# Starting the state space tables' small operations 20 steps earlier, in the first half of the values' product

## The chip, the cores and the metric

One Trainium2 chip, one of its cores. The metric is the device time of one execution in microseconds (us). Before the change it is 940.51 us, the median of 3 runs from 940.02 to 942.69. Engine names in the rows: PE is TensorE (PEld its weight loads), DVE is VectorE, ACT is ScalarE, POOL is GpSimd, SPq is SyncE's DMA queue.

## What is computed

One layer of an encoder on 512 tokens of 1024 channels. The parts that matter here:

```python
xn = rmsnorm(h, norm_mix)
proj = xn @ w_in                       # channels for S5, pooling, q, k, v, gates
u_s5, u_pool, qkv, gate_logits = split(proj)

dt = exp(log_dt)[:, None]              # S5: 64 rows (2 directions x 32 groups) of 64 states
a_bar = exp(lam * dt)                  # complex
b_bar = ((a_bar - 1.0) / lam)[:, :, None] * b
# a scan over time with a_bar, then a product with c

scores = einsum('bdiqhe,bdikhe->bdihqk', q, k) - slopes * dist
p = exp(scores - max(scores))          # dilated attention, 16 heads
```

Behind them follow the merge of the three branches by their gates, an output projection and a two-layer network.

## The kernel before

**Products in three matmuls.** Every float32 operand of a large product is split into a high part (a rounded copy) and a low part (the difference), and `mm3` (lines 121 to 123) adds high x high, high x low and low x high. ScalarE makes the high half of a weight piece (`wh`, line 96), VectorE the low half (`wl`, line 103). Weight pieces are loaded by SyncE into three raw buffers (line 181). The load into a buffer is issued right behind the low split that empties it, in program order, so SyncE waits there for that split. Each of `wh` and `wl` has two buffers.

**Steps.** The order of all work is the order in which the program issues it, engine by engine. A clock counts steps: `tick()` (line 136) is called after each `mm3` group and issues what is due: first the calls put off with `later(n, f)`, then one portion of each generator in `background`. `use(i)` (line 235), called as a product reaches weight piece `i`, puts off the split of piece `i + 1`: its high half by two steps, its low half by three. `finish()` (line 154) ticks until no generator is left, without any matmul in between.

**The stretch of the change.**
- Steps 1 to 32: first half of the values' product (`tokmajor(P_v[0], ...)`, line 695). Its left operand is x scaled by the norm's gains, not yet by the rows' factors; `v_ahead` (line 441) splits x for a later channel block, and at `k == 1` (step 4) starts the generator `norm1`. Here `k` counts channel blocks of four steps, so `k == 3` is called with the clock at 12.
- `norm1` (line 383): loads x by rows (until step 11), squares them on ScalarE (steps 19 to 26), makes the rows' factors `rows_rs` on GpSimd (step 27), broadcasts them on VectorE (30) and transposes the broadcast on TensorE (step 32, line 409). From step 34 to 58 it does, for each of eight channel blocks in three steps each, a product on VectorE (`nx`: line 106), a copy on ScalarE (`xh`) and a difference on VectorE (`xl`).
- Steps 33 to 64: second half of the values' product (line 699). Low splits of weight pieces are issued in steps 35, 43, 51 and 59; the one of step 51 is first used in step 57, the one of step 59 by the first S5 unit.
- Steps 65 to 88: three units of the S5 input projection (line 719), eight steps each, with low splits in steps 67, 75 and 83. Steps 89 to 104: the units for k and q of the first two heads, whose results VectorE and ScalarE evict (`k_done`, `q_done`). Steps 105 to 108: half of the fourth S5 unit. Then `finish()` (line 956), the loads of the first two score bias tables T (`load_T`, line 751) and of the S5 tables; then the attention loop.

**The list of the change.** `s5_prep()` (line 450) makes the S5 tables: about 110 operations, nearly all on VectorE and on 64 partitions. It does not issue them as it runs; it records them with an estimated cost and then plays the list back, a portion per step:

```python
for cost, f in ops:
    if cost is None:
        spent = 0.0
        yield f
        continue
    f()
    spent += cost
    if spent > PACE:
        spent = 0.0
        yield
```

`PACE` is 0.35, so two small operations (0.2 or 0.22) go out per step, or one wide one. The order in the list: three loads and a pause of 8 steps; an exponential on 64 x 1 (15 operations); the products with dt and the two reduced angles; an exponential on 64 x 64 (15); two sines on ScalarE and a pause of 3; powers of a_bar by complex products of growing width (64 x 64 to 64 x 512); the factor (a_bar - 1) / lam; two products and two sums on 64 x 1024 or half of it; four stores to DRAM; eight loads; a pause of 16 (`PREP_WAIT`); 19 transposes on TensorE; their evictions; and six operations on 128 x 512 (`Bb`). Each score tile adds the bias table T on VectorE (line 770), and the softmax rows are normalised by GpSimd (line 109) before TensorE transposes them (line 797).

Of the kernel before, what the change touches and what calls it, by code (L numbers as in the profile page):

```python
# [55 lines left out]
def trunk(ctx: ExitStack, tc: tile.TileContext, a: dict, out):  # L56
# [7 lines left out]
    def fr(t):  # L64
        return t.bitcast(F32)
# [10 lines left out]
    def z(dt=F32, n=512):  # L76
        t = z_p.tile([128, 512], dt, tag="z", name="z")
        return t if n == 512 else t[:, 0:n]
# [4 lines left out]
    def ps():  # L83
        return ps_p.tile([128, 512], F32, tag="ps", name="ps")

    def sm(n=1):
        t = small.tile([128, 4], F32, tag="sm", name="sm")
        return t[:, 0:n]
# [5 lines left out]
    def copy(eng, o, i, scale=1.0):  # L94
        if eng is SE:
            SE.activation(out=o, in_=i, func=AF.Copy, scale=scale)  # L96
        elif scale != 1.0:
            eng.tensor_scalar(out=o, in0=i, scalar1=scale, scalar2=1.0, op0=MUL, op1=MUL)
        else:
            eng.tensor_copy(out=o, in_=i)  # L100

    def tt(o, i, j, op, eng=None):
        (eng or VE).tensor_tensor(out=o, in0=i, in1=j, op=op)  # L103

    def stt(o, i, s, j, op0, op1):
        VE.scalar_tensor_tensor(out=o, in0=i, scalar=s, in1=j, op0=op0, op1=op1)  # L106

    def ts(o, i, s1, s2, op0, op1, eng=None):
        (eng or VE).tensor_scalar(out=o, in0=i, scalar1=s1, scalar2=s2, op0=op0, op1=op1)  # L109
# [22 lines left out]
    def later(n, f):  # L132
        clock[1] += 1
        put_off.append((clock[0] + n, clock[1], f))
# [16 lines left out]
    def start(gen):  # L151
        background.append([clock[0] + 1, gen])
# [194 lines left out]
    def split_xT(k):  # L347
        h, l = xg_h[k], xg_l[k] = zr(), zr()
        g = gT[:, k:k + 1]
        SE.activation(out=h, in_=xT[k], func=AF.Copy, scale=g)  # L350
        stt(l, xT[k], g, fr(h), MUL, SUB)
# [31 lines left out]
    def norm1():  # L383

        xs = []
        for t in range(4):
            for hf in range(2):
                x = z()
                SP.dma_start(out=x, in_=a["x"][t * 128:t * 128 + 128, 512 * hf:512 * hf + 512])
                xs.append(x)  # L390
            yield 2
        yield 6
        for i, x in enumerate(xs):
            SE.activation(out=x, in_=x, func=AF.Square, accum_out=rows_ss[:, i % 2, i // 2:i // 2 + 1])
            yield 1
        s2 = sm(4)
        tt(s2, rows_ss[:, 0], rows_ss[:, 1], ADD, GE)
        ts(s2, s2, 1.0 / D, EPS, MUL, ADD, GE)
        mh4 = mhalf.to_broadcast([128, 4])
        tt(rows_rs, s2, mh4, ALU.pow, GE)  # L400
        yield 3
        rb = z()
        for t in range(4):
            ts(rb[:, t * 128:t * 128 + 128], ones, rows_rs[:, t:t + 1], 1.0, MUL, MUL)
        yield 2
        p = ps()
        for t in range(4):
            o = slice(t * 128, t * 128 + 128)
            TE.transpose(p[:, o], rb[:, o], ident)
        yield 1  # L410
        copy(SE, R, p)
        yield 1
        for k in range(8):
            stt(xT[k], xT[k], gT[:, k:k + 1], R, MUL, MUL)
            yield 1
            copy(SE, xT_h[k], xT[k])
            yield 2
            tt(xT_l[k], xT[k], fr(xT_h[k]), SUB)
# [3 lines left out]
    def v_evac(t, hf, p):  # L422
        vt[t][hf] = z()
        SE.activation(out=vt[t][hf], in_=p, func=AF.Copy, scale=rows_rs[:, t:t + 1])

    def tokmajor(P, lhs_h, lhs_l, ahead=None):

        acc = [ps() for _ in range(4)]
        ks = [(pi, i) for pi in P for i in range(pieces[pi][0].shape[1])]
        for k, (pi, i) in enumerate(ks):  # L430
            if i == 0:
                hs, ls = use(pi)
            if ahead:
                ahead(k)
            for t in range(4):
                o = slice(t * 128, t * 128 + 128)
                mm3(acc[t], lhs_h[k][:, o], lhs_l[k][:, o], hs[i], ls[i], k == 0, k == len(ks) - 1)
                tick()
        return acc

    def v_ahead(k):
        if k < 6:
            later(1, lambda: split_xT(k + 2))
        if k == 1:
            start(norm1())


    s5c = []
# [226 lines left out]
    def unit_quanta(pi, hT, lT, done, ks=range(8), sub=None):  # L675
# [17 lines left out]
        return [lambda i=i: quantum(i) for i in range(n)]  # L693

    acc0 = tokmajor(P_v[0], xg_h, xg_l, v_ahead)
    for t in range(4):
        later(1 + t, lambda t=t: v_evac(t, 0, acc0[t]))
    start(s5_prep())
    acc = tokmajor(P_v[1], xg_h, xg_l)
    for t in range(4):  # L700
        later(1 + t, lambda t=t: v_evac(t, 1, acc[t]))
# [933 lines left out]
```

## Time and profile before

| | us |
|---|---|
| median of 3 runs | 940.51 (940.02 to 942.69) |
| the profiled execution | 939.83 |
| its span, first to last instruction | 938.0 |
| TensorE busy | 918.2 (98%) |
| VectorE busy | 586.3 (63%) |
| ScalarE busy | 444.7 (47%) |
| GpSimd busy | 308.0 (33%) |

All rows come from the profiled execution, which was 0.68 us below the median; the span leaves out the 1.8 us around its first and last instruction. Busy shares are means over stages with different limits. A row of a timeline has the start, the length, the engine, the line of the kernel, the operation, the tiles written and read, a count and, in brackets, the idle time of the engine before it with what ended it. The length of a short row overlaps the next one: what an operation costs its engine is the distance from start to start. TensorE's granted clock stands as a fraction of 2.4 GHz; it is 1.00 in every row that is shown here.

### The profile page before, as it was taken

Reading aid. Unit: us, or ns where it says so; the run is one execution under the profiler, and the core shown is the slowest. Engines: PE = TensorE matmul, PEld = TensorE weight load, DVE = VectorE, ACT = ScalarE, POOL = GpSimd, SP = SyncE. Lnnn points to the kernel's source line nnn. Section 1 sums busy time; section 2 is a strip of 40 time slices with the busy share of each in tenths; the row PEclk is TensorE's granted clock in tenths of the full one; section 3 lists DMA queues with packets and bytes.
Section 4 is the critical chain, followed back from the end, with each engine's and each line's share of the span. In section 5 each row is a group of like instructions: output and inputs, shape, how many; then the busy total and the mean of one; then the engine's idle time right before and its main releaser. Section 6 shows DMA issues by size and latency. Waiting matters only on the chain.

```text
span 938.0 us, 12750 instructions
## 1 busy us (share of the span) xinstructions
PE 918.2 (98%) x4683; PEld 736.6 (79%) x4683; DVE 586.3 (63%) x921; ACT 444.7 (47%) x711; POOL 308.0 (33%) x416
## 2 busy tenths in 40 slices
PE   9999999999999999999999999999999999999997
PEld 6878776777777888878888878888888888888876
DVE  4698788887544765567754564436665857675443
ACT  5544765667654334444444332345444444444522
POOL 0000465557788883022100000056034314501302
PEclk9999999999999999999999999999999999999999
DMA  9237766642313334454352254281333134221222
GB/s 323 85 116 204 200 180 168 161 120 87 103 48 100 94 101 124 107 127 115 108 152 63 73 179 135 68 268 47 107 116 115 53 96 154 82 66 45 67 90 90
DMA packets 140462, 111.05 MB, mean 118 GB/s; under 512 B 16368, under 2 KB 117104, under 8 KB 140400
## 3 DMA queue, kind: packets, MB, share of 16 engines
q1 hardware_dynamic: 140400, 110.24, 39.6%
q8 instruction: 37, 0.61, 0.3%
q14 instruction: 25, 0.20, 0.1%
HBM read 106.32 MB, written 3.90 MB: 117 GB/s over the span
## 4 chain that ended last, share of the span: by engine, by line
PE 80%; DVE 11%; ACT 4%; issue 2%; DMA 1%; SPq 0%; POOLq 0%; DVEq 0%; POOL 0%; ACTq 0%
PE ps L121 20%; PE ps L122 20%; PE ps L123 20%; PE ps L1461 4%; PE ps L1462 4%; PE ps L1460 4%; DVE z L103 3%; PE ps L813 2%; DVE wl L103 2%; ACT z L96 2%; DVE z L106 2%; PE ps L797 2%; DVE S L770 1%; ACT wh L96 1%; PE ps L1131 1%
## 5 line engine op out<-in xcount | busy, mean ns | idle before, releaser
L103 DVE TENSOR_TENSOR wl<-raw,wh 128x1024 fp32r<-128x1024 f32 (+1 forms) x113 | 152.8, 1354 | 171.8 <-ACT wh L96 171.0
L121 PE MATMUL ps<-xh,wh 128*128 128x512 f32 x384 | 156.5, 407 | 0.2 <-ACT wh L96 0.2
L123 PE MATMUL ps<-xh,wl 128*128 128x512 f32 x384 | 150.3, 391 | 0.9 <-DVE wl L103 0.9
L122 PE MATMUL ps<-xl,wh 128*128 128x512 f32 x384 | 149.7, 390 | 0.0
L96 ACT ACTIVATE wh<-raw 128x1024 fp32r<-128x1024 f32 (+1 forms) x112 | 117.5, 1049 | 34.4 <-issue 9.3
L96 ACT ACTIVATE z<-ps 128x512 f32<-128x512 f32 (+4 forms) x128 | 72.8, 579 | 67.9 <-PE ps L123 25.2
L122 PE MATMUL ps<-hl,wh 128*128 128x512 f32 (+1 forms) x272 | 102.5, 377 | 0.3 <-DVE hl L103 0.3
L121 PE MATMUL ps<-hh,wh 128*128 128x512 f32 (+1 forms) x272 | 102.5, 377 | 0.3 <-ACT hh L96 0.3
L123 PE MATMUL ps<-hh,wl 128*128 128x512 f32 (+1 forms) x272 | 102.4, 376 | 0.0
L109 POOL TENSOR_SCALAR S<-S,sm 128x512 f32<-128x512 f32 x64 | 61.2, 974 | 97.6 <-ACT wh L96 78.4
L123 PEld LDWEIGHTS ps<-xh,wl 128*128 128x128 f32 x384 | 72.1, 188 | 17.0 <-DVE wl L103 1.3
L121 PEld LDWEIGHTS ps<-xh,wh 128*128 128x128 f32 x384 | 72.4, 189 | 14.9 <-issue 0.9
L122 PEld LDWEIGHTS ps<-xl,wh 128*128 128x128 f32 x384 | 72.4, 189 | 12.7
L1361 ACT ACTIVATE R<-ps 128x512 f32<-128x512 f32 x32 | 19.2, 598 | 128.0 <-PE ps L123 128.0
L103 POOL TENSOR_TENSOR z<-z 128x512 f32<-128x512 f32 x24 | 38.0, 1599 | 122.0 <-DVE z L106 75.8
L777 ACT ACTIVATE S<-S,sm 128x512 f32<-128x512 f32 x64 | 46.2, 722 | 53.9 <-DVE sm L109 52.2
L1460 PE MATMUL ps<-wh,ah 128*128 128x512 f32 x168 | 65.4, 389 | 0.0
L1461 PE MATMUL ps<-wh,al 128*128 128x512 f32 x168 | 65.4, 389 | 0.0
L1462 PE MATMUL ps<-wl,ah 128*128 128x512 f32 x168 | 65.4, 389 | 0.0
L109 POOL TENSOR_SCALAR sm<-sm 128x1 f32<-128x1 f32 (+1 forms) x16 | 3.6, 225 | 175.9 <-ACT hn L1331 148.1
L103 POOL TENSOR_TENSOR B<-B,B 128x1024 f32<-128x1024 f32 x18 | 50.4, 2820 | 27.9 <-DVE wl L103 16.1
L122 PEld LDWEIGHTS ps<-hl,wh 128*128 128x128 f32 x272 | 51.2, 188 | 10.0 <-DVE hl L103 0.5
(208 smaller groups left out, 1900.4 us busy)
## 6 DMA issues: line engine op xcount, KB each, us to landing
raw<-in_w_in_dram SPq DMA_DIRECT2D x55, 512.0 KB
raw<-in_w_up_dram SPq DMA_DIRECT2D x32, 512.0 KB
B<-in_w_down_dram SPq DMA_DIRECT2D x24, 512.0 KB
T<-in_ttab_dram SPq DMA_DIRECT2D x16, 448.0 KB
z<-Fd SPq DMA_DIRECT2D x16, 256.0 KB
raw<-in_w_branch_attn_dram SPq DMA_DIRECT2D x8, 512.0 KB
raw<-in_w_out_dram SPq DMA_DIRECT2D x8, 512.0 KB
raw<-in_w_down_dram SPq DMA_DIRECT2D x8, 512.0 KB
```

Of the source, the lines that this page charges most:

```text
L96: SE.activation(out=o, in_=i, func=AF.Copy, scale=scale)
L103: (eng or VE).tensor_tensor(out=o, in0=i, in1=j, op=op)
L106: VE.scalar_tensor_tensor(out=o, in0=i, scalar=s, in1=j, op0=op0, op1=op1)
L109: (eng or VE).tensor_scalar(out=o, in0=i, scalar1=s1, scalar2=s2, op0=op0, op1=op1)
L121: TE.matmul(o, wh, xh, start=first, stop=False)
L122: TE.matmul(o, wh, xl, start=False, stop=False)
L123: TE.matmul(o, wl, xh, start=False, stop=last)
L777: SE.activation(out=s, in_=s, func=AF.Exp, bias=nm, accum_out=den[h][:, t:t + 1])
L1361: SE.activation(out=r, in_=p, func=AF.Relu)
L1460: TE.matmul(acc[t], ah[:, k, o], hs[i], start=st, stop=False, **kw)
L1461: TE.matmul(acc[t], al[:, k, o], hs[i], start=False, stop=False, **kw)
L1462: TE.matmul(acc[t], ah[:, k, o], ls[i], start=False, stop=sp, **kw)
```

## The change

The generator `s5_prep` is started by `v_ahead` at channel block 3 of the first half of the values' product, with the clock at 12, and no longer between the two halves, with the clock at 32. Nothing else differs; the list, its pauses and its pace are the same.

```diff
@@ -443,6 +443,8 @@
             later(1, lambda: split_xT(k + 2))
         if k == 1:
             start(norm1())
+        if k == 3:
+            start(s5_prep())
 
 
     s5c = []
@@ -695,7 +697,6 @@
     acc0 = tokmajor(P_v[0], xg_h, xg_l, v_ahead)
     for t in range(4):
         later(1 + t, lambda t=t: v_evac(t, 0, acc0[t]))
-    start(s5_prep())
     acc = tokmajor(P_v[1], xg_h, xg_l)
     for t in range(4):
         later(1 + t, lambda t=t: v_evac(t, 1, acc[t]))
```

## Rows read from the trace of the kernel before

**Rows 1.** Busy time by 10 us: engines, granted clock, DMA share, GB/s.

```profile
20.00:30.00 10.00, 10.00 (x48) 8.31 (x47) 3.96 (x7) 7.00 (x19) 1.78 (x3) 1.00 0.62 212
...
40.00:50.00 10.00, 9.17 (x41) 7.27 (x40) 9.45 (x32) 3.48 (x5) 0.00 (x0) 1.00 0.31 91
```

**Rows 2.** TensorE's timeline, 40 to 62 us: start, length, instruction, [idle before, its releaser].

```profile
47.47 0.50 PE L122 MATMUL ps<-wl,z 128*128 128x512 f32 x1 [0.83 <-DVE wl L103]
...
54.78 0.51 PE L123 MATMUL ps<-xh,wl 128*128 128x512 f32 x1 [0.87 <-DVE wl L103]
...
60.37 0.39 PE L123 MATMUL ps<-xh,wl 128*128 128x512 f32 x1
```

**Rows 3.** Who waited for whom, TensorE, 0 to 200 us: total, times, longest.

```profile
PE ps L797 <- POOL S L109: 2.5, 7, 0.7
```

**Rows 4.** VectorE's timeline, 20 to 40 us.

```profile
25.73 1.23 DVE L103 TENSOR_TENSOR wl<-raw,wh 128x1024 fp32r<-128x1024 f32 x1 [3.26 <-ACT wh L96]
28.44 0.88 DVE L109 TENSOR_SCALAR z<-ones,rows_rs 128x128 f32<-128x128 f32 x4 [1.49 <-POOL rows_rs L103]
30.73 0.75 DVE L106 SCALAR_TENSOR_TENSOR z<-z,gT,R 128x512 f32<-128x512 f32 x1 [1.41 <-ACT R L96]
32.26 1.23 DVE L103 TENSOR_TENSOR wl<-raw,wh 128x1024 fp32r<-128x1024 f32 x1 [0.78 <-ACT wh L96]
...
35.45 0.69 DVE L103 TENSOR_TENSOR xl<-z,xh 128x512 fp32r<-128x512 f32 x1 [0.70 <-ACT xh L96]
...
38.45 1.23 DVE L103 TENSOR_TENSOR wl<-raw,wh 128x1024 fp32r<-128x1024 f32 x1 [1.04 <-ACT wh L96]
```

**Rows 5.** VectorE's timeline, 40 to 75 us.

```profile
46.21 1.21 DVE L103 TENSOR_TENSOR wl<-raw,wh 128x1024 fp32r<-128x1024 f32 x1
...
53.52 1.21 DVE L103 TENSOR_TENSOR wl<-raw,wh 128x1024 fp32r<-128x1024 f32 x1
...
56.66 0.19 DVE L476 MEMSET P<- 64x64 f32 x2
...
56.95 1.21 DVE L103 TENSOR_TENSOR wl<-raw,wh 128x1024 fp32r<-128x1024 f32 x1
...
59.81 0.42 DVE L103 TENSOR_TENSOR m<-P,sg 64x256 f32<-64x256 f32 x1
...
65.56 0.22 DVE L103 TENSOR_TENSOR sp<-sp,sp 64x64 f32<-64x64 f32 x1
...
72.13 2.44 DVE L103 TENSOR_TENSOR Fw<-m,m 32x1024 f32<-32x1024 f32 x2
```

**Rows 6.** SyncE's queue, 0 to 112 us.

```profile
17.30 0.94 SPq L389 DMA_DIRECT2D z<-in_x_dram  x2
...
86.63 1.06 SPq L753 DMA_DIRECT2D T<-in_ttab_dram  x2
```

**Rows 7.** Timeline of all engines, 26 to 31 us.

```profile
27.39 1.02 POOL L103 TENSOR_TENSOR rows_rs<-sm,mhalf 128x4 f32<-128x4 f32 x1
...
29.46 0.60 PE L409 MATMUL ps<-ident,z 128*128 128x128 f32 x4
```

**Rows 8.** Table operations on small tiles (sp) alone, 45 to 56.7 us.

```profile
45.00:56.70 11.70, 5.64 (x29) 0.39 (x2) 1.00 0.21 60
```

**Rows 9.** TensorE's timeline, 84 to 91 us.

```profile
84.75 1.16 PE L607 MATMUL ps<-ident,m 64*128 64x64 f32 x16
...
90.30 0.40 PE L767 MATMUL ps<-kz,z 128*128 128x512 f32 x1
```

**Rows 10.** VectorE's timeline, 92 to 125 us.

```profile
92.85 0.68 DVE L770 CUSTOM_DVE_ANT_0 S<-ps,T 128x512 f32<-128x512 f32 x1
...
120.92 1.66 DVE L103 TENSOR_TENSOR wl<-raw,wh 128x1024 fp32r<-128x1024 f32 x1
```

**Rows 11.** Busy time, GB/s last, as the tables for the first scores load.

```profile
87.00:90.00 3.00, 3.00 (x15) 2.47 (x14) 2.94 (x12) 1.08 (x2) 0.00 (x0) 1.00 0.82 260
90.00:91.00 1.00, 1.00 (x6) 0.79 (x5) 0.96 (x3) 0.98 (x3) 0.00 (x0) 1.00 0.99 373
```

## The prediction

> **What bounds the kernel now.** I first read the busy time in stretches of 10 us [rows 1]. TensorE is full from 20 to 30 us and loses 0.83 us from 40 to 50; VectorE goes the other way, 3.96 us busy in the first stretch and 9.45 in the second. So VectorE sets the pace in the second, and has room in the first. TensorE's own timeline shows what the loss is [rows 2]: it waits for the low half of a weight piece (a `wl` that VectorE makes), 0.83 us before 47.47 and 0.87 us before 54.78. The split after those two is early: its first use is at 60.37. Up to 200 us the list of waits names one other large item, transposes that wait for softmax rows normalised on GpSimd, 2.5 us in seven waits [rows 3]. Then VectorE's timeline: before 40 us its gaps, with the engine that ended each [rows 4], and the saturated stretch behind [rows 5]. An engine works in the order of issue, so what follows is a running account of one queue.
>
> **What is removed and added: nothing.** The same instructions are issued; the list of table operations starts 20 steps earlier (after step 12, not 32; a step is three matmuls, 0.68 us). Its three loads go out in step 13, its VectorE work starts in step 21 (before: 41) and it ends in step 102 (before: 122). The last 14 of the old steps held no matmul: `finish()` ran them after step 108.
>
> **Steps 21 to 30: hidden.** Eighteen small operations fall here, about 3.1 us, twelve before the `wl` at 25.73 and six after it. The gaps there are 3.26 and 1.49 us [rows 4]. They fit, if the loads have landed. On SyncE's queue these stand after the last x loads, issued from 17.30 to 18.24 [rows 6], so they are out by 20. The transfers ahead of them keep the DMA engines busy for about half of the stretch from 20 to 30 (share 0.62 [rows 1]); if all move in order of issue, the loads land near 23.3 us, and I take 0. If they land last, at 24.5, the eighteen end about 0.6 us late, and TensorE waits that long for the broadcast it transposes at 29.46 [rows 7].
>
> **Steps 30 to 64: the main term.** I go from one `wl` to the next and ask how late it is against before.
> - To the `wl` of step 43 (38.45). Steps 30 to 42 now carry 26 small operations instead of 4. Twenty-nine of them took 5.64 us busy, 0.194 each [rows 8], and with the gap to the next, some 0.02, one costs 0.215: 5.6 us in place of 0.7. The gaps they meet are 1.41, 0.78, 0.70 and 1.04, 3.9 us [rows 4]. Some 0.5 us of these stay idle, because the ScalarE copies that end them are bound to TensorE or to VectorE's own output. Late: 5.6 - 0.7 - 3.9 + 0.5 = 1.5 us; I take 1.4, as some operations overlap a neighbour.
> - To the `wl` of step 51 (46.21). Twelve operations: those that ran from 56.66 to 59.81 before [rows 5], less one `wl` of 1.14 from start to start, 2.0 us, and one more of 0.2; the list's pause for the sine leaves 0.5 idle. Before there were 16: 38.45 to 46.21 is 7.76 us, less a `wl` of 1.14 and three pairs of norm operations of 1.26 each, leaves 2.8. Late: 1.4 - 0.1 = 1.3 us. TensorE waits for this piece already, so it waits **1.3 us** more.
> - To the `wl` of step 59 (53.52). Ten operations, the wide ones of the powers among them, those from 59.81 up to 65.56 without its `wl` and the gap ahead of it, 3.85 us; before 16 operations in 7.31 - 1.14 - 3.12 = 3.05 us. With 0.2 for overlaps, late: 1.3 + 0.8 - 0.2 = 1.9 us. TensorE is itself 1.3 us late by now: **0.6 us** more.
> - To the `wl` of step 67 (56.95). Fifteen operations, those from 65.56 to 72.13 less one `wl`, 5.4 us; before 12 in 3.43 - 1.14 = 2.3 us. Late: 1.9 + 3.1 = 5.0 us. This piece had a margin: done at 58.16, wanted at 60.37 [rows 2], 2.2 us. 5.0 - 2.2 - 1.9 = **0.9 us**, a new wait.
>
> The `wl` after that comes just as TensorE asks for it; then the list pauses, and VectorE is idle again. Sum 2.8 us. Bounds: 1.2 (less than half of each lateness is real, the operations running closer together) to 3.4 (the next `wl` 0.6 late as well).
>
> **Steps 68 to 108 and the queue behind them.** The DMAs that the list issues (four table stores, eight loads) enter SyncE's queue in steps 68 to 75, ahead of weight loads that are needed 8 steps later or more: 0. The 19 transposes of the tables move from after step 108 to steps 91 and 92, some 1.4 us of TensorE in either place [rows 9], with inputs ready 10 us before: 0.
> What is left is a trade. Before, VectorE worked on the list's rest right up to 92.85, where the first score of the attention starts [rows 10]; its matmul was done at 90.7 [rows 9], so it was 2.15 us late. That goes. But six operations of 0.65 us now stand among the k and q evictions of steps 96 to 105, and about 1.25 us of them does not fit the gaps. With the transposes ahead, the `wl` of step 107 comes 1.4 + 1.25 = 2.65 us later against TensorE. SyncE's next weight load waits for that `wl`, and behind it in the queue stands the score's bias table, issued at 86.63 before [rows 6]. Nothing waited for that table; it is what is late next. When does it land? The piece ahead of it is 524 KB, the table 459 KB. From 87 to 90 us 260 GB/s moved 780 KB, then 373 GB/s [rows 11]: in order of issue the table is done at 90.54. Plus 2.65 is 93.2 on the old clock, against 92.85: 0.35 us later. If it lands 0.9 us sooner, 0.6 us are won; if it shares the engines with the second table and both end at 91.9, 1.7 us are lost. The softmax waits [rows 3] follow one to one. I take **0.35 us**, the value of the rows, with -0.6 and +1.7 for the range.
>
> **Sum.** 2.8 + 0.35 = 3.1 us. Against the profiled execution, 939.83 us, that is 942.9 us. The median is 0.68 us above this execution, so the forecast is **943.6 us**, 0.33% slower. A measurement of this kernel can tell about 0.3%, 2.8 us, from no change: the forecast lies at that edge.
>
> **Where the Trainium skill has a word.** The three GpSimd operations that make `rows_rs`, the last of 1.02 us at 27.39 [rows 7], ran with VectorE idle for all but the first 0.4 us; now six small operations run beside them. A `wl` beside GpSimd work took 1.66 us at 120.92 [rows 10], one without it 1.21 us at 46.21 [rows 5]: the two engines can hold each other up. If each of the three is held for one operation of 0.215 us, `rows_rs` is 0.65 late; the broadcast made from it was ready 0.1 us before TensorE took it, so TensorE loses 0.55 and the time is 944.2.
> The Trainium skill, SBUF — State Buffer, section "Who interferes with whom", says that a VectorE instruction with two SBUF inputs contends with a GpSimd instruction that reads SBUF, and that the loser is blocked for the whole instruction. By it the sum is the 944.2 of this mechanism; by the rows of before, which have no such pair at this place, it is 943.6.
>
> **The rivals.**
> 1. *The stalls grow, and the softmax waits shrink* (0.38). The bias table lands as soon as the score's matmul is done; the scores start 2.15 us earlier against TensorE, and 1.9 of the 2.5 us of waits [rows 3], those of the first two heads, go: 2.8 - 1.9 = +0.9 us, 941.4. For it: these waits follow the late scores. Against it: the order in SyncE's queue. If instead the 2.8 us are short by half, the time is within 0.3% as well.
> 2. *The early gaps take it all* (0.06), which gives a faster kernel. The place is the `wl` of step 43: if it is no later than before, the work taken out of the stretch ahead of the second half's pieces frees VectorE, and the waits of [rows 2], 2.4 us from matmul to matmul, vanish with the softmax's 1.9: 936.2. It decides when steps 30 to 42 hold less than 4.1 us of small operations; I count 5.6.
> 3. *GpSimd is held* (0.08): 944.2, as above.
> 4. *The change does not do what it says* (0.05): the loads land so late, or a buffer comes free so late, that the list runs where it did. 940.5.
>
> The forecast's own case has 0.43. Slower by over 0.3% is that and rival 3, 0.51; within 0.3% are rivals 1 and 4, 0.43; faster 0.06. The range: below, rival 1 with the main term at its lower end, 1.2 - 1.9, gives 939.8, of which I take 940.2; above, 3.4 + 1.7 and 0.6 for late loads, 5.7 us, gives 946.2, and with a little of rival 3, 946.4.
>
> **What would show it.** Right: the first table operation on VectorE near 23 us; almost no idle VectorE between 30 and 42; the `wl` of 46.21 near 47.5; TensorE's waits about 1.3 and 0.6 us larger, and a new one of 0.9 us near 62; no block of table work after step 108, and VectorE idle before the first score. Wrong: a wait before the transposes near 29.5 (late loads, or GpSimd held), the `wl` of step 43 still at 38.5, or a first score that starts as its matmul ends.

## The result, and the profile after

The changed kernel takes **945.87 us** (943.25 to 947.26, 6 runs) beside 940.0 us of the kernel before (938.68 to 942.69, 6 runs): 1.0058 times as long, 95% interval 1.0041 to 1.0074. The forecast was 943.6 us, so the direction is right, the time lies in the range, and the size is short by 2.3 us. The profiled execution took 945.67 us, 5.84 more than the one of before. The page's head:

```profile
span 943.9 us, 12751 instructions
...
PE 921.9 (98%) x4683; PEld 737.5 (78%) x4683; DVE 587.2 (62%) x921; ACT 444.4 (47%) x711; POOL 307.5 (33%) x416
```

TensorE is busy 3.7 us longer with the same 4683 instructions; that alone says that part of the loss is no wait. The busy time by 10 us, the view of [rows 1] (columns as there):

```profile
20.00:30.00 10.00, 10.00 (x47) 8.11 (x45) 6.62 (x26) 7.12 (x19) 2.32 (x3) 1.00 0.53 174
30.00:40.00 10.00, 10.00 (x46) 8.28 (x46) 8.98 (x33) 6.01 (x10) 0.00 (x0) 1.00 0.31 98
40.00:50.00 10.00, 8.19 (x36) 6.33 (x36) 9.26 (x23) 3.14 (x7) 0.00 (x0) 1.00 0.20 54
50.00:60.00 10.00, 8.34 (x31) 6.15 (x30) 9.59 (x28) 5.47 (x8) 0.00 (x0) 0.87 0.37 104
...
70.00:80.00 10.00, 10.00 (x57) 7.88 (x56) 4.59 (x14) 3.05 (x4) 0.00 (x0) 1.00 0.99 266
```

VectorE's work came forward (3.96 us in [rows 1], now 6.62, between 20 and 30), yet it is as full as before from 40 to 60, and free only from 70 on. TensorE loses 1.81 us from 40 to 50, where it lost 0.83. And in the fourth row its granted clock is 0.87. TensorE's timeline, the answer to [rows 2]:

```profile
48.86 0.50 PE L122 MATMUL ps<-wl,z 128*128 128x512 f32 x1 [1.81 <-DVE wl L103]
56.77 0.51 PE L123 MATMUL ps<-xh,wl 128*128 128x512 f32 x1 [1.58 <-DVE wl L103]
```

The two waits of 0.83 and 0.87 us have grown to 1.81 and 1.58. A third, near 62, is missing. The reason stands in the busy time by single us; the column ahead of the last two is the granted clock:

```profile
57.00:58.00 1.00, 1.00 (x4) 0.82 (x4) 0.93 (x5) 0.64 (x2) 0.00 (x0) 0.70 0.14 20
58.00:59.00 1.00, 1.00 (x4) 0.71 (x4) 0.90 (x5) 0.00 (x0) 0.00 (x0) 0.50 0.87 237
59.00:60.00 1.00, 1.00 (x4) 0.81 (x3) 0.90 (x4) 0.00 (x0) 0.00 (x0) 0.50 0.87 260
60.00:61.00 1.00, 1.00 (x5) 0.77 (x4) 1.00 (x2) 0.00 (x0) 0.00 (x0) 0.60 0.08 14
...
112.00:113.00 1.00, 1.00 (x4) 0.79 (x3) 0.97 (x2) 0.00 (x0) 0.06 (x1) 0.50 1.02 320
```

Behind the second wait TensorE ran at 0.50, which is 1.2 in place of 2.4 GHz, from 57.4 to 60.8 us, and once more from 112.0 to 115.4. A step from one matmul to the next is 0.425 us there, in place of 0.227, as between these two on TensorE's timeline:

```profile
58.14 0.63 PE L121 MATMUL ps<-xh,wh 128*128 128x512 f32 x1
58.56 0.63 PE L122 MATMUL ps<-xl,wh 128*128 128x512 f32 x1
```

A stretch of 3.4 us holds eight: 8 x 0.198 = **1.6 us** lost. Neither stretch is in the trace of before, which has one of its own near 552 us. VectorE's timeline, for [rows 4, 5]:

```profile
24.84 0.15 DVE L109 TENSOR_SCALAR sp<-ldt 64x1 f32<-64x1 f32 x1 [2.24 <-DMA ldt<-in_s_log_dt_dram]
...
26.95 1.23 DVE L103 TENSOR_TENSOR wl<-raw,wh 128x1024 fp32r<-128x1024 f32 x1
...
29.18 0.86 DVE L109 TENSOR_SCALAR z<-ones,rows_rs 128x128 f32<-128x128 f32 x4
...
40.03 1.23 DVE L103 TENSOR_TENSOR wl<-raw,wh 128x1024 fp32r<-128x1024 f32 x1 [0.43 <-ACT wh L96]
47.60 1.21 DVE L103 TENSOR_TENSOR wl<-raw,wh 128x1024 fp32r<-128x1024 f32 x1
55.50 1.21 DVE L103 TENSOR_TENSOR wl<-raw,wh 128x1024 fp32r<-128x1024 f32 x1
61.89 1.21 DVE L103 TENSOR_TENSOR wl<-raw,wh 128x1024 fp32r<-128x1024 f32 x1
```

The low halves of steps 43, 51, 59 and 67 are later than before by 1.58, 1.39, 1.98 and 4.94 us; foretold were 1.4, 1.3, 1.9 and 5.0. The first table operation waited for its load until 24.84. On GpSimd's timeline, beside [rows 7]:

```profile
27.17 1.91 POOL L103 TENSOR_TENSOR rows_rs<-sm,mhalf 128x4 f32<-128x4 f32 x1
```

It took 1.91 us in place of 1.02, beside the low split of 26.95. The transposes of the tables on TensorE, for the block of [rows 9], then the bias table's issue on SyncE, for [rows 6], and the first score on VectorE, for [rows 10]:

```profile
76.77 0.66 PE L609 MATMUL ps<-ident,m 64*128 64x64 f32 x8
...
78.25 0.71 PE L609 MATMUL ps<-ident,m 64*128 64x64 f32 x8
```

```profile
93.71 1.05 SPq L754 DMA_DIRECT2D T<-in_ttab_dram  x2
```

```profile
98.92 0.69 DVE L771 CUSTOM_DVE_ANT_0 S<-ps,T 128x512 f32<-128x512 f32 x1 [5.64 <-DMA T<-in_ttab_dram]
```

VectorE stood idle for 5.64 us before the first score, until the table was there, 5.2 us after its issue. The waits that follow on TensorE, with line 797 now line 798 [rows 3]:

```profile
109.38 0.33 PE L798 MATMUL ps<-ident,S 128*128 128x128 f32 x1 [1.18 <-POOL S L109]
110.05 0.33 PE L798 MATMUL ps<-ident,S 128*128 128x128 f32 x1 [0.34 <-POOL S L109]
...
111.38 0.33 PE L798 MATMUL ps<-ident,S 128*128 128x128 f32 x1 [0.34 <-POOL S L109]
```

Four of them, 2.2 us; the first head had 0.92 before. **Where 5.8 us went** is read by setting each matmul beside the same one of before:

| up to | TensorE later by, us | what was added |
|---|---|---|
| the norm's transposes (29.8) | 0.31 | `rows_rs` late; 0.13 of it stands already ahead of them |
| the first wait (48.86) | 1.39 | 1.08, low half of step 51 |
| the second wait (56.77) | 1.98 | 0.59, low half of step 59 |
| 61 us | 3.6 | 1.6, half clock |
| the first matmul behind steps and transposes (90.13) | 4.29 | 0.7, transposes in two blocks |
| behind the first head's waits (112.0) | 6.1 | 1.8, of which 1.3 are the waits |
| 115.4 us | 7.6 | 1.5, half clock again |
| 558.5 us | 7.4 | second head without its waits, -1.4; third head +1.2 |
| 562.8 us and to the end | 5.8 | the kernel before has a half-clock stretch of its own there, -1.6 |

### The profile page after: what moved, and what is told of

Read it like the earlier page. It is cut to its first block, busy times and chain, and to the rows that moved or that the text cites. A ratio compares the mean times of both kernels' runs of the same rounds, so it can differ in the third digit from the quotient of the medians.

```text
span 943.9 us, 12751 instructions
## 1 busy us (share of the span) xinstructions
PE 921.9 (98%) x4683; PEld 737.5 (78%) x4683; DVE 587.2 (62%) x921; ACT 444.4 (47%) x711; POOL 307.5 (33%) x416
## 4 chain that ended last, share of the span: by engine, by line
PE 78%; DVE 13%; DMA 3%; ACT 3%; issue 2%; SPq 0%; POOL 0%; POOLq 0%; DVEq 0%; ACTq 0%
PE ps L121 19%; PE ps L123 19%; PE ps L122 19%; PE ps L1463 4%; PE ps L1461 4%; PE ps L1462 4%; DVE z L103 4%; DVE wl L103 2%; PE ps L814 2%; DVE z L106 2%; PE ps L798 2%; DVE S L771 2%; ACT z L96 1%; PE ps L1132 1%; ACT wh L96 1%
## 5 line engine op out<-in xcount | busy, mean ns | idle before, releaser
L778 ACT ACTIVATE S<-S,sm 128x512 f32<-128x512 f32 x64 | 46.2, 722 | 56.8 <-DVE sm L109 55.3
L103 DVE TENSOR_TENSOR z<-z 128x512 f32<-128x512 f32 (+1 forms) x68 | 53.3, 790 | 10.7 <-DMA z<-in_w_glu_dram 6.6
```

Of the source, the lines that this page charges most:

```text
L778: SE.activation(out=s, in_=s, func=AF.Exp, bias=nm, accum_out=den[h][:, t:t + 1])
```

## The experiments

Each kernel ran beside the kernel before on the same chip. Ratios are to that, with 95% intervals. The clock is the mean over all runs of a kernel; a stretch at half clock lowers it by about 0.0018 (half of 3.4 us in 944). In the last column are the stretches of the profiled run after its first 20 us and before 550 us.

| kernel | us | ratio | clock | waits on low halves, 40 to 66 us | first head's softmax waits | half clock |
|---|---|---|---|---|---|---|
| after, first runs | 945.87 | 1.0058 [1.0041, 1.0074] | 0.9937 | 1.81, 1.58 | 2.2 | 57.4; 112.0 |
| after_again | 945.62 | 1.0059 [1.0044, 1.0074] | 0.9948 | 1.79, 1.58 | 2.2 | 58.8; 113.4 |
| tail_back | 943.06 | 1.0035 [1.0018, 1.0051] | 0.9959 | 1.80, 1.58 | 0.9 | 57.8 |
| bias_first | 942.23 | 1.0025 [1.0010, 1.0041] | 0.9967 | 1.80, 1.58, 0.65 | 0.2 | none |
| loads_early | 945.83 | 1.0053 [1.0034, 1.0072] | 0.9943 | 1.79, 0.32, 0.62 | 2.2 | 51.8; 113.3 |
| split_early | 945.65 | 1.0066 [1.0048, 1.0083] | 0.9953 | 0.53 (and 2.28 on a high half) | 2.2 | 56.8; 111.4 |
| hold_20 | 941.14 | 1.0011 [0.9998, 1.0024] | 0.9969 | 0.42, 0.90 | 0.9 | none |
| two_parts | 938.11 | 0.9986 [0.9971, 1.0002] | 0.9972 | 0.61 | 0.9 | none |
| t_late | 940.68 | 1.0005 [0.9987, 1.0022] | 0.9968 | 0.84, 0.86 | 0.9 | none |
| t_later | 942.86 | 1.0036 [1.0023, 1.0048] | 0.9946 | 0.83, 0.87 | 2.2 | 110.3 |
| best | 938.85 | 0.9990 [0.9978, 1.0001] | 0.9972 | 0.23 | 0.2 | none |
| best2 | 938.99 | 0.9985 [0.9968, 1.0002] | 0.9970 | 0.23 | 0.2 | 115.6 |
| best3 | 937.09 | 0.9967 [0.9955, 0.9979] | 0.9973 | none | 0.3 | none |

The kernel before had 939.6 to 940.1 us in these comparisons, and a mean clock of 0.9971 to 0.9976.

### Undoing the second half of the change: tail_back and bias_first

`tail_back` is the changed kernel with the end of the list (transposes, evictions, `Bb`) put back to where it was:

```diff
-PREP_WAIT = 16
+PREP_WAIT = 36
```

> The list starts early as in the changed kernel, but its pause ahead of the transposes is 36 steps, so that the transposes, their evictions and the six operations on 128 x 512 run after step 108 again, as before the change. Theory (two separate costs: low splits that come late in steps 43 to 67, and bias tables that are loaded late because the tail of the list pushes the low split of step 107): the waits near 48.9 and 56.8 us stay at 1.8 and 1.6 us, and TensorE's clock may fall to half behind them; the first score starts from VectorE's queue and not from the landing of its bias table; the first softmax wait falls from 2.2 us in sum to about 0.9, and the half clock near 112 us goes. That is 3 us less than the changed kernel, near 943 us, +0.3% on before. Rival (the tail costs nothing, all of the loss is the late low splits and what follows from them): no change against the changed kernel, +0.6%.

`bias_first` leaves the list, and issues the bias tables' loads ahead of the last half unit instead, so that no weight load stands before them:

```diff
-    run(qs[:4])
     finish()
     PT, Bb, A8 = s5c
     prep_p.release()
     att_p = tc.alloc_tile_pool(name="att", bufs=1, side="right", reuse_waits="tile")
     load_T(0)
     load_T(1)
+    run(qs[:4])
```

> The changed kernel with the end of the list, the release of its tiles and the loads of the first two bias tables put ahead of the fourth S5 unit (step 104), so that in SyncE's queue they stand ahead of the weight load that waits for the low split of step 107. Theory: the tables are issued some 4 us earlier, near 89.6 us; the first score starts within 0.3 us of its matmul's end (it waited 3.9 us for its table in the changed kernel); the first softmax waits, 2.2 us, and the half clock behind them, 1.6 us, go: 3.8 us less than the changed kernel, near 942 us, +0.2% on before. Rival (the softmax waits are paced by GpSimd and not by the table): the table comes earlier and the waits stay at 2.2 us, +0.6% on before.

943.06 and 942.23 us. In both the low halves' waits are those of the changed kernel, and the first head's softmax waits are back at 0.9 us or below it; with them went the stretch at half clock near 112. Against the changed kernel's 1.0058 that is 0.23% and 0.33%: the late bias table, and what hangs on it, is worth 2 to 3 us, and the list's early part, which is left in both, again 2 to 3 us. In the trace of `bias_first` no clock fell near 57, with the same two waits ahead as in `tail_back`, where it did; over their runs the mean clock is 0.9967 and 0.9959. So these waits do not bring the clock down in every run. Where it stayed up the foretold third wait shows, on TensorE's timeline:

```profile
48.80 0.50 PE L122 MATMUL ps<-wl,z 128*128 128x512 f32 x1 [1.80 <-DVE wl L103]
...
56.70 0.50 PE L123 MATMUL ps<-xh,wl 128*128 128x512 f32 x1 [1.58 <-DVE wl L103]
...
63.09 0.50 PE L123 MATMUL ps<-xh,wl 128*128 128x512 f32 x1 [0.65 <-DVE wl L103]
```

This matmul stood at 60.37 in [rows 2]: 2.72 us later, where the sum of the main term was 2.8.

### Only the first operations early: hold_20

```diff
         ts_(th, lim, dt, 1.0, MUL, MUL)
+        pause(20)
```

> The changed kernel with a pause of 20 steps after the eighteenth small operation: those eighteen run in VectorE's gaps of steps 21 to 30, and the rest runs from step 50, exactly where it ran before the change. Theory (the harm is the work moved into steps 30 to 64; the gaps before are free): the low splits of steps 43 and 51 come no later than before, the waits near 47.5 and 54.8 us (0.83 and 0.87) fall to under 0.5 us together, no half clock near 57 us, the part after step 108 as before: 2 us less than before, near 938 us, -0.2%. Rival (the late landing of the list's loads, or table work beside GpSimd near 27 us, is what makes the second half slow): the waits stay at 1.8 and 1.6 us and the time at +0.4% or more.

941.14 us: a miss. The list resumes at step 50. TensorE's timeline:

```profile
49.44 0.50 PE L122 MATMUL ps<-wl,z 128*128 128x512 f32 x1 [0.42 <-DVE wl L103]
55.23 0.50 PE L121 MATMUL ps<-xh,wh 128*128 128x512 f32 x1 [0.27 <-ACT wh L96]
56.87 0.50 PE L123 MATMUL ps<-xh,wl 128*128 128x512 f32 x1 [0.90 <-DVE wl L103]
```

The first wait halved, the second did not: between the low halves of steps 51 and 59 VectorE carried sixteen small operations, as many as before, and the second low half came 7.44 us after the first, against 7.31. Eighteen operations taken out ahead do not help where the rest is as dense as it was. Why the median is not even 0.4 us lower than before stays open; its interval reaches to 0.9998.

### Two parts: two_parts

```diff
         if k == 1:
             start(norm1())
-        if k == 3:
             start(s5_prep())
...
+        pause(27)
         exp_to(er, xre, 64)
```

> The list starts with norm1 (step 4), its loads go out in step 5, its first thirty operations run in steps 13 to 28, and after a pause of 27 steps the second exponential runs from step 56, where it ran before the change; the rest is as before the change. Theory: as for the pause of 20, with more taken out of steps 41 to 55 (5.8 us of VectorE instead of 3.1): both waits near 47.5 and 54.8 us go but for some 0.2 us, 2.2 to 2.4 us less than before, near 937.8 us, -0.25%. Rival (loads placed among the first x loads hold up the row factors): a wait before the transposes near 29.5 us and a time at or above before.

938.11 us. The loads are out at step 5; the first exponential and the angles run in VectorE's gaps, and the rest from step 56, behind most of the norm's products. One wait is left:

```profile
55.05 0.50 PE L123 MATMUL ps<-xh,wl 128*128 128x512 f32 x1 [0.61 <-DVE wl L103]
```

1.1 us of waits went, and the time fell by 2.0, short of what its interval can tell from no change. Beside `tail_back`, which also leaves the list's end behind step 108, it is 5.0 us less: of two lists that both start early, the one whose middle part stays out of steps 30 to 55 costs nothing that can be told.

### The changed kernel again, and two of its parts: after_again, loads_early, split_early

`after_again` has no edit.

> The changed kernel once more, unaltered, beside the three below. Theory (VectorE's queue sets the size: late low halves 2.5 us, softmax waits 1.3 us): waits of 1.8 and 1.6 us near 48.9 and 56.8 us again, a third of about 0.65 us near 63 us unless TensorE has a stretch at half its granted clock just ahead of it, and a median of 943.5 to 944.5 us, mean clock as of the kernel before (0.997). Rival (the longer waits bring TensorE's clock down: the first six runs of the changed kernel had a mean clock of 0.994, the kernel before 0.997): a stretch of 3.4 us at half clock behind the waits in this trace too, a mean clock of 0.994 again, and a median near 946 us.

945.62 us, with both stretches at half clock again and a mean clock of 0.9948: the rival was right, the clock belongs to the result. The profiled run, 947.02 us, has a third stretch, from 14.4 to 17.8 us.

`loads_early`:

```diff
         if k == 1:
             start(norm1())
-        if k == 3:
             start(s5_prep())
...
-        pause(8)
+        pause(16)
```

> The changed kernel with the list's three loads issued in step 5 in place of 13 and the pause behind them 16 steps in place of 8, so that the table work still begins in step 21. Theory (the late landing of the loads costs only at the transposes): first table operation near 22.5 us in place of 24.8, the transposes near 29.8 back by 0.3 us, the waits of 1.8 and 1.6 us as they are within 0.3: 0.3 us less than the changed kernel. Rival (the late loads push the whole list back, and the late low halves come from there): the first waits fall to about 0.9 us, and the time by 1.5 us or more.

The waits stayed (1.79; the second is smaller because the half clock came ahead of it in this run). The first table operation waited for no load, the transposes came without delay, and on GpSimd's timeline stands the reason:

```profile
29.65 1.02 POOL L103 TENSOR_TENSOR rows_rs<-sm,mhalf 128x4 f32<-128x4 f32 x1
```

But `after_again`, with the loads where the change has them, shows the same there:

```profile
29.08 1.02 POOL L103 TENSOR_TENSOR rows_rs<-sm,mhalf 128x4 f32<-128x4 f32 x1
```

In both traces TensorE had lost 1.6 us at half clock from 14.3 or 14.4 us on, so every step behind it came later; in `after_again` the first table operation waited 0.48 us for its load, not 2.24. So this pair does not show that the earlier loads brought the transposes back. `best`, below, has the early loads, no stretch near 14 and the 1.02 us, but its list also starts earlier. In time it is 945.83 against 945.62 us, nothing that can be told. Shown is that the late loads are no cause of the late low halves: without any wait for a load the first wait was still 1.79 us.

`split_early`:

```diff
-        d = SPLIT_AT
+        d = 0 if 30 <= clock[0] <= 64 else SPLIT_AT
```

> The changed kernel with the splits of the pieces used from step 41 to 72 issued two steps earlier (both halves); the list is where the change put it. The low half of step 51 then passes two norm operations and the table work between them, about 2 us of VectorE's queue, that of step 59 about 1.8 us, that of step 67 about 2.6 us. Theory (these low halves stand too far back in VectorE's queue): the wait of 1.8 us goes to about 0, that of 1.6 us stays near 1.5 us, since TensorE asks 1.8 us sooner, and there is no third one: 2 to 2.5 us less than the changed kernel beside it. Rival (the waits are of ScalarE's high halves or of the raw loads, and VectorE only comes last): the waits stay within 0.4 us of 1.8 and 1.6, and the time within 0.5 us of the changed kernel.

945.65 us: a miss. The wait near 48.9 is gone, but then TensorE and ScalarE show these rows (and, at 69.20, a third wait of 0.64 us for a low half, where none was foretold):

```profile
54.50 0.50 PE L121 MATMUL ps<-xh,wh 128*128 128x512 f32 x1 [2.28 <-ACT wh L96]
55.76 0.50 PE L123 MATMUL ps<-xh,wl 128*128 128x512 f32 x1 [0.53 <-DVE wl L103]
```

```profile
52.87 0.63 ACT L96 ACTIVATE xh<-z 128x512 fp32r<-128x512 f32 x1 [1.74 <-DVE z L106]
53.41 1.99 ACT L96 ACTIVATE wh<-raw 128x1024 fp32r<-128x1024 f32 x2
```

The high half stands on ScalarE behind a copy that waits 1.74 us for VectorE's norm product. So ScalarE keeps VectorE's pace here: to move the low half up moves the wait from one half to the other. By this run what counts is the work that VectorE has to do by step 59, and not the place of the low half in it.

### The bias table alone, in the kernel before: t_late and t_later

Both are edits of the kernel before; the list stays where it was. `t_late`:

```diff
-    def load_U(j):
+    def load_U(j, mid=None):
...
         for s in range(8):
+            if mid and s == 4:
+                mid()
...
-    load_T(0)
-    load_T(1)
-    W_load(0)
+    Ut[0] = load_U(0, lambda: (load_T(0), load_T(1)))
+    FB[0] = s5_W_load(0, 0)
```

> The kernel before (the list where it was), with the first two bias tables' loads moved behind four of the eight loads of U that follow them in SyncE's queue: issued about 2.4 us later, near 89 us, landed near 94 us, where the first score now starts at 92.85. In the changed kernel that score is at 98.9, which is 94.6 on the old clock. Theory (a late bias table alone lengthens the first head's softmax waits, and TensorE's clock falls for a stretch right behind them): first score 1 to 2 us late, those waits 1.9 to 2.9 us in place of 0.9, a stretch of 3.4 us at half clock near 108 to 113 us, low halves' waits of 0.8 and 0.9 us as before: 1 to 2 us plus 1.6, 942.5 to 943.5 us. Rival 1 (the clock falls behind late low halves only, or by chance): the waits grow, but no half-clock stretch near 110: 941 to 942 us. Rival 2 (the late table is not what delays the scores): first score at 92.9 as before, 940 us.

940.68 us: rival 2. SyncE's queue and VectorE:

```profile
89.40 0.90 SPq L755 DMA_DIRECT2D T<-in_ttab_dram  x2
```

```profile
93.29 0.68 DVE L772 CUSTOM_DVE_ANT_0 S<-ps,T 128x512 f32<-128x512 f32 x1
```

Issued 2.3 us later on the old clock (this run is 0.5 us behind from its start), the table landed within 3.9 us and nobody waited. `t_later` puts the loads behind all eight:

```diff
-    load_T(0)
-    load_T(1)
-    W_load(0)
+    Ut[0] = load_U(0)
+    load_T(0)
+    load_T(1)
+    FB[0] = s5_W_load(0, 0)
```

> The kernel before, with the first two bias tables' loads behind all eight loads of U, issued near 92.5 us: later than with four of them, where the tables came in time all the same. At 3.8 us or less from issue to use they are there near 95.5 to 96.3 us, and the first score starts 2.5 to 3.2 us later than at 92.85. Theory (late bias tables lengthen the softmax waits one to one, and the clock falls for a stretch behind them): the first head's waits 3.0 to 4.0 us in place of 0.9, a stretch of 3.4 us at half clock between 108 and 115 us, and 2 to 3 us plus 1.6 more time: 943.5 to 945 us. Rival (the waits grow, but no clock falls; it belongs to the list's place): 942 to 943 us without such a stretch near 110.

942.86 us. VectorE waits for the table, TensorE for the softmax rows, and then the clock falls, with the list where it was before the change:

```profile
98.31 0.69 DVE L770 CUSTOM_DVE_ANT_0 S<-ps,T 128x512 f32<-128x512 f32 x1 [2.71 <-DMA T<-in_ttab_dram]
```

```profile
100.38 0.50 PE L123 MATMUL ps<-xh,wl 128*128 128x512 f32 x1 [1.01 <-DVE wl L103]
108.74 0.33 PE L797 MATMUL ps<-ident,S 128*128 128x128 f32 x1 [1.18 <-POOL S L109]
```

```profile
110.00:111.00 1.00, 0.58 (x3) 0.39 (x3) 0.00 (x0) 0.98 (x3) 1.00 (x3) 0.64 1.04 311
111.00:112.00 1.00, 1.00 (x4) 0.81 (x4) 0.67 (x1) 0.30 (x1) 1.00 (x2) 0.50 0.20 56
```

The waits are 2.2 us, not the 3 to 4 foretold, and another 1.0 for a low half that stood on VectorE behind the waiting score; the rival, no fall of the clock, is out by the trace, though the median lies where the rival put it. The profiled run is the slowest of the nine (945.18 us) and has two more stretches at half clock, near 14.7 and 557.4 us; but the mean clock of all nine is 0.9946, as in the changed kernel, beside 0.9973 of the kernel before.

### A better version: best, best2, best3

`best` is `two_parts` with the edits of `split_early` and `bias_first`, and the list's end earlier:

```diff
-PREP_WAIT = 16
+PREP_WAIT = 4
```

> The list's loads in step 5, its first part (the small exponential, the products with dt, the angles) in the idle time of VectorE up to step 30, a pause of 27 steps ahead of the second exponential, a pause of 4 in place of 16 ahead of the transposes, the bias tables' loads issued ahead of the last half unit, and the splits of steps 41 to 72 two steps earlier. Theory: the one wait left by the two-part list (0.61 us near 55) goes, and the first two heads' softmax waits fall by about 1.5 us, because VectorE is done with the table work when the first score comes: 935.5 to 936.5 us, 0.4% below the kernel before. Rival (the table work moved 12 steps up, between the evictions of k and q, makes low halves late there): a new wait of TensorE between 70 and 90 us, and 938 us or more.

938.85 us: the wait near 55 fell to 0.23, the first two heads' waits by 0.7 us only (the second head kept 1.0), and the rival came true beside it. With `finish()` ahead of the half unit, all that was left of the list ran on VectorE before the next low half, and TensorE waited 1.4 us for that near 89 us. `best2` tried to move that split, and joined the transposes:

```diff
-        d = 0 if 30 <= clock[0] <= 64 else SPLIT_AT
+        d = 0 if 30 <= clock[0] <= 64 or 96 <= clock[0] <= 106 else SPLIT_AT
...
             rec(0.0, lambda i=i: tr(i))
-            pause(1)
```

> The kernel best with the last half unit's split two steps earlier too (steps 97 to 108), past two of the wide table operations, and the tables' 19 transposes in one block in place of two. Theory (what best lost behind its gain was that low half, for which TensorE waited 1.4 us near 89 us, and 0.7 us for the second block of transposes): no wait over 0.3 us between 70 and 95 us, 1.5 to 2 us less than best, 936.8 to 937.4 us. Rival (the half unit's split is held by the evictions, not by the table work): the wait stays over 1 us, and the time within 0.5 us of best's 938.9.

938.99 us, and the wait is 1.58 us: a miss. By the program `finish()` moves the clock past 106 before that split is due, so the edit met another one (78.62 us in `best`, 76.73 here), and the one in question stayed behind the list. `best3` is `two_parts` with the edit of `split_early`, and half of `Bb` on GpSimd:

```diff
-            tt_(v3(b2), v3(b2), bq(1), MUL, 0.6)
-            tt_(o, v3(b1), bq(0), MUL, 0.6)
-            tt_(o, o, v3(b2), ADD, 0.6)
+            eng = GE if dd == 0 else VE
+            rec(0.6 * dd, lambda o=v3(b2), j=bq(1), eng=eng: tt(o, o, j, MUL, eng))
+            rec(0.6 * dd, lambda o=o, i=v3(b1), j=bq(0), eng=eng: tt(o, i, j, MUL, eng))
+            rec(0.6 * dd, lambda o=o, j=v3(b2), eng=eng: tt(o, o, j, ADD, eng))
```

> The two-part list as it ran above, with the splits of steps 41 to 72 two steps earlier, and three of the six last wide operations of the list (the first half of Bb) on GpSimd, which is idle from 70 to 100 us, in place of VectorE. Theory: the wait of 0.61 us near 55 goes down to about 0.2, VectorE reaches the first score near 91.8 us in place of 93.1, about when the bias table lands, and the first two heads' softmax waits fall by 1.3 us in sum or more: 1.5 us less than the two-part list, 936.3 to 937.0 us. Rival (VectorE's three others are held by GpSimd's, or the bias table lands only near 92.9): the first score stays within 0.4 us of 93, the time at 937.5 to 938.5 us.

**937.09 us, 0.9967 [0.9955, 0.9979]**: faster than both kernels, and just above the 936.3 to 937.0 us foretold. No low half is waited for between 40 and 75 us, and VectorE is at the first score at 91.86 [rows 10]:

```profile
88.69 0.41 DVE L622 COPY PT<-ps 128x256 f32<-128x256 f32 x1
89.05 1.57 DVE L103 TENSOR_TENSOR z<-z,fs 128x512 f32<-128x512 f32 x1
...
90.54 0.68 DVE L103 TENSOR_TENSOR Bb<-z,fs 128x512 f32<-128x512 f32 x1
...
91.86 0.68 DVE L772 CUSTOM_DVE_ANT_0 S<-ps,T 128x512 f32<-128x512 f32 x1
```

```profile
88.78 1.29 POOL L103 TENSOR_TENSOR Bb<-Bb,z 128x512 f32<-128x512 f32 x1
```

The first two heads' waits fell by 0.7 us, not 1.3, and nearly half of the 1.9 us that were moved came back: the product at 89.05 took 1.57 us, not 0.68, for as long as GpSimd's sum ran beside it. A new wait of 0.66 us stands at the norm's transposes (31.30 us), behind an x load for which ScalarE waited 1.35 us; in `two_parts`, with the same loads, there is none, and its cause was not tried.

## Why the prediction was right, and where its size was off

- **Main term, 2.8 us: right.** Low halves late by 1.39, 1.98 and 4.94 us (foretold 1.3, 1.9, 5.0), waits greater by 0.98 and 0.71, and the third one 0.65 where the clock stayed up; together with some 0.3 us at the transposes 2.72 us (`bias_first`). The gaps did not take the work (rival 2), because steps 30 to 42 held more than VectorE's idle time there. `split_early` adds what the account left out: ScalarE's high halves hang on the same queue.
- **Loads at 23.3 us, price 0: wrong by 0.2 us in the profiled run.** The first operation waited until 24.84, and TensorE lost 0.2 us at the transposes, with 0.13 of its 0.31 us there already ahead of them. The step that failed is "if all move in order of issue"; the loads came near the other bound, 24.5. In `after_again`, whose TensorE was later by then, it cost nothing.
- **Rival 3, GpSimd held: its mechanism is there, by another pair.** `rows_rs` took 1.91 us beside the low split that the late operations had pushed to 26.95 (1.97 to 2.10 us in `tail_back`, `bias_first` and `split_early`); in `after_again` and `loads_early` the split was past and it took 1.02. That split ended at 28.18, and 1.02 us behind that is later than 29.08, where `rows_rs` ended, so the small operations added nothing that shows. Nor is it right that the rows of before have no such pair: the first of the three operations took 0.56 us at 26.46, beside the low split of 25.73, and 0.20 us in the changed kernel, ahead of the split. The Trainium skill, SBUF — State Buffer, section "Who interferes with whom", names VectorE instructions with two SBUF inputs as those that contend with a GpSimd instruction that reads SBUF. These rows agree, as does `best3`, where such an instruction went from 0.68 to 1.57 us, while the copy from PSUM ahead of it kept its 0.41 us.
- **Transposes, price 0: wrong by 0.7 us.** Before, the 19 stood in one block of 1.33 us behind step 108. Among the steps the list's pause of one step parts them into two, which push TensorE back by 2.0 us in sum; "some 1.4 us in either place" overlooked the pause.
- **The bias table, 0.35 us: the mechanism right, the size off.** It was issued 2.8 us later on the old clock, for 2.65 foretold. The landing was taken at 3.9 us, in order of issue; it took 5.2, as the upper bound had it (both tables done together, +1.7). Applied to before, 5.2 us from 86.63 gives 91.8, 1 us ahead of the score: so 1.8 us late, and the softmax waits rose by 1.3, less than one to one. That three transfers share the engines is argued from the bytes (the piece of 524 KB and two tables of 459, 1.44 MB; 1.35 MB had moved from 94 to 98.9 us); shown is that without a weight load right ahead the table was used 3.9 us behind its issue (`t_late`, nobody waiting) and 4.0 (`t_later`, 94.28 to 98.31).
- **The clock: not in the sum.** The prediction has no term for it and gives no reason; 1.00 in the rows of before was taken to hold for after. Each stretch costs 1.6 us. The one near 112 came in all 5 profiled runs with 2.2 us of softmax waits and in 1 of the 9 with shorter ones; the one near 57 in 5 of the 6 with the longer waits on weight halves there (in `loads_early` after the first of them alone), and in none of the 8 others. That is company and not yet cause; `t_later`, where a late table alone brought the waits and a mean clock as low as the changed kernel's, is the one test. The early stretch took the place of the third wait, so it is 1.0 us net. With the second, the extra 1.0 at the table and the 0.7 of the transposes, this makes up the 2.3 us missed and more; the kernel before has a stretch of its own to set against it, and the early one was not in every run. That the time lies in the range is therefore in part luck: the range was made wide for late loads, a late table and GpSimd, and no bound of it held the clock.
- Rival 1 (the softmax waits shrink) held for the second head alone, by 1.4 us, of which the third gave back 1.2. Rival 4 is out: the list ran where the diff puts it.

## What to carry to other kernels

Work taken forward on an in-order engine helps only if the gaps it meets hold all of it; otherwise its rest sits ahead of the next thing that the bottleneck waits for, so split the list where the gaps end (`two_parts`, `best3`). Price a load by what stands right ahead of it in the queue. And a few waits of TensorE, 1.8 and 1.6 us here, can cost another 1.6 us in clock behind them, though not in every run: look at the granted clock of each stretch, not at the waits alone.

## What the chip showed that was not expected

TensorE's granted clock fell to 0.50 (1.2 GHz) for 3.4 us at a time, 1.6 us lost each time: behind the waits of 1.8 and 1.6 us on low halves in most profiled runs, and behind the 2.2 us of softmax waits in all of them. The kernel before has such a stretch too, from 552.3 to 555.8 us, and waits stand right ahead of it:

```profile
551.12 0.51 PE L121 MATMUL ps<-wh,z 128*128 128x512 f32 x1 [1.16 <-ACT wh L96]
552.38 0.80 PE L122 MATMUL ps<-wl,z 128*128 128x512 f32 x1 [0.76 <-DVE wl L103]
```

These two waits, 1.14 to 1.18 and 0.75 to 0.77 us, are in all 14 traces, and the clock fell behind them in six; in the profiled run of the changed kernel they stand at 558.49 and 559.75, and it did not. Five runs have a stretch from near 14.5 us on, behind waits of 0.75 to 1.31 and 0.76 us. The end of the slow first microseconds varied from 4.0 to 10.2 us between profiled runs. What decides whether the clock falls behind the same waits was not tried. These stretches may be part of why single runs of one kernel differ by up to 8 us.
